# Second-layer modulation as sums on VectorE, and a router that multiplies before the norm, in a two-layer hybrid block with experts

## The chip, the core and the metric

The kernel runs on one core of a Trainium2 chip. The metric is the device time of one execution in microseconds (us); smaller is better. All data are 32-bit floats. The engines that matter here are TensorE (PE; its weight loads are listed as PEld), VectorE (DVE), ScalarE (ACT), GpSimd (POOL) and SyncE (SP), which issues almost all transfers. Each engine works through its own queue in order.

## What is computed

Two layers act on 256 latent tokens and 256 context tokens of width 1024. Cut to what the change touches:

```python
silu_c, silu_cc = silu(c), silu(c_ctx)                     # one vector of 1024 for each stream
m_lat = split(silu_c  @ mod_w[i] + mod_b[i], 6)            # mod_w[i]: 1024 x 6144, 25 MB a layer
m_ctx = split(silu_cc @ mod_w[i] + mod_b[i], 6)
z_lat = modulate(rmsnorm(x, norm1_g[i]), m_lat[0], m_lat[1]) @ w_in[i]
x = x + m_lat[2] * merge(z_lat, att_lat)                   # mixer: pooling, Hyena, attention, w_out
# layer 0: dense SwiGLU on both streams.  layer 1: experts on the latents alone:
u = modulate(rmsnorm(x, norm2_g[1]), m_lat[3], m_lat[4])   # u = x * r * a + b
logits = u @ router_w                                      # 1024 x 8; top 2 of 8 experts for each token
x = x + m_lat[5] * experts(u, logits)
```

The last layer needs the context stream only for its first norm, so of its six modulation vectors only shift and scale of the mixer (column tiles 0 to 3 below) are used for both streams.

## The kernel before

Activations lie transposed: `self.x[j]` holds stream j (0 latents, 1 context) as eight blocks of 128 features by 256 tokens. A product in full precision is made of three products of split operands (`three`, L269): a weight block `raw` (128x1024) is loaded, ACT rounds it to `wh` (L262) and DVE subtracts to get `wl` (L263), and TensorE then runs 24 matmuls of 128x512 for one block (L272 to L274), called a projection here. The ring of `raw` tiles has seven buffers and is shared with the modulation weights (`modw`, same tag); `wh` and `wl` have four buffers each, so weights are prepared up to three projections ahead. PSUM has three tags: `mm` (3 buffers), `aux` (2), `sc` (3).

The modulation weights of a layer are 12 column tiles of 512, each loaded as four chunks (q = 0 to 3) of 128x1024 (two slices of 128 input features, k). In a chunk, four matmuls with the 32 columns of `cvec` as stationary operand (silu of c, silu of c_ctx and zeros) and 256 weight columns moving go to four column groups of the array (`modulation_part`, L353). After the fourth chunk of a tile, `modulation_row` copies the sums to SBUF on ACT (L360), transposes them in two blocks on TensorE (L363), and adds halves and bias on DVE (L367, L369) into `modT`. Ten tiles of layer 0 are done before and inside the first mixer. The last two of layer 0 and all twelve of layer 1 are `self.chunks`: 56 chunks, of which `mod_chunk` takes one after each projection of the dense SwiGLU. There `up` makes gate and up projections for 22 feature blocks, and `down` (called after blocks 8 and 16 and at the end) runs eight output blocks, whose sums DVE adds to both streams (L839).

After the second mixer, `to_experts` (L1363) computes the affine, the norm `r` (`rstd`: Ln, Exp and Square on ACT, three operations on DVE), then eight blocks `xf[k]` = x * r * a + b (DVE L1369; the second step on ACT L1371 for k < 5, on DVE L1373 for the rest), and `logits` multiplies them by the router in four column groups (L915), copies the sums (L917), transposes them (L920) and adds the groups (L923). `route` finds the top two (L935 to L948), `token_major` transposes `xf`, `gather` collects each expert's tokens (L1038), and `experts` streams 336 MB of expert weights through 16 buffers (`mraw`) with the matmuls of L1136, L1147, L1177 and L1185.

The order on each engine is made by a scheduler when the program is built. It follows data dependences and buffer reuse, so the listings of order further down show what it chose.

Of the kernel before, what the change touches and what calls it, by code (L numbers as in the profile page):

```python
# [18 lines left out]
F32 = mybir.dt.float32  # L19
# [3 lines left out]
OP = mybir.AluOpType  # L23
AX = mybir.AxisListType

P = 128
D = 1024
KD = D // P
L = 256
# [5 lines left out]
NE = 8  # L35
EPS = 1e-6
MAGIC = 1.5 * 2.0 ** 23
PAD = 8
# [157 lines left out]
class Trunk:  # L196
# [130 lines left out]
    def conditioning(self):  # L327

        nc = self.nc
        lo = self.par_at["c"][0]  # L330
        both = self.pars[:, lo:lo + 2 * KD]
        sc = self.keep.tile([P, 2 * KD], F32, name="silu_c")
        nc.scalar.activation(sc, both, AF.Exp, scale=-1.0)
        nc.vector.tensor_scalar(sc, sc, 1.0, None, op0=OP.add)
        nc.vector.reciprocal(sc, sc)
        nc.vector.tensor_mul(sc, sc, both)
        self.cvec = self.pre.tile([P, KD, 32], F32, name="cvec")
        nc.gpsimd.memset(self.cvec, 0.0)
        for j in range(2):
            nc.vector.tensor_copy(self.cvec[:, :, j], sc[:, j * KD:(j + 1) * KD])  # L340
# [51 lines left out]
    def mod_chunk(self):  # L392

        if not self.chunks:
            return
        l, ct, q = self.chunks.pop(0)
        if q == 0:
            self.mod_ps = self.sc()
        self.modulation_part(self.mod_ps, q, self.modulation_load(l, ct, q))
        if q == 3:  # L400
            self.modulation_row(l, ct, self.mod_ps, self.aux)

    def mod_chunks_until(self, l, ct):
        while self.chunks and self.chunks[0][:2] < (l, ct):
            self.mod_chunk()
# [499 lines left out]
        down(16, 6, then)  # L905


    def logits(self, xf):

        nc = self.nc  # L910
        ps = self.sc(L)
        rw = self.par("router").rearrange("p (k e) -> p k e", k=KD)
        for k in range(KD):
            g = 32 * (k % 4)
            nc.tensor.matmul(ps[g:g + 32], rw[:, k], xf[k], start=k < 4, stop=k >= 4, tile_position=(0, g))  # L915
        parts = self.tmp("t2", w=L)
        s = nc.scalar.copy(parts, ps)  # L917
        pt = self.sc(L)
        for t in range(2):
            m = nc.tensor.transpose(pt[:, t * P:(t + 1) * P], parts[:, t * P:(t + 1) * P], self.ident)  # L920
        self.routed = m.ins, s.ins
        lg = self.keep.tile([P, 2, NE], F32, name="lg")
        nc.vector.tensor_reduce(lg, pt.rearrange("p (t g e) -> p t e g", t=2, g=4)[:, :, :NE], axis=AX.X, op=OP.add)  # L923
        return lg

    def route(self, lg, between):
# [376 lines left out]
    def run(self, upto=99):  # L1303
        nc, tc = self.nc, self.tc
        with ExitStack() as es:
            self.load(es)
            with ExitStack() as pre:
# [37 lines left out]
                nxt = {}  # L1345
# [15 lines left out]
                xf = []  # L1361

                def to_experts(j):  # L1363
                    a, b = self.affine(1, 2)
                    r = self.norm(0)
                    pairs = [self.block(f"v{k}", T) for k in range(4)]
                    xf.extend(pairs[k // 2][:, k % 2 * L:(k % 2 + 1) * L] for k in range(KD))
                    for k in range(KD):
                        v = nc.vector.tensor_mul(xf[k], self.x[0][:, k], r)  # L1369
                        if k < 5:  # L1370
                            s = nc.scalar.activation(xf[k], xf[k], AF.Identity, bias=b[:, k, 0:1], scale=a[:, k, 0:1])  # L1371
                        else:
                            v = nc.vector.tensor_scalar(xf[k], xf[k], a[:, k, 0:1], b[:, k, 0:1], op0=OP.mult, op1=OP.add)  # L1373
                    nxt["xf"] = v.ins, s.ins
                    nxt["lg"] = self.logits(xf)

                self.merge(0, ym, T, to_dense)
                self.dump("x1", [x[:, k] for x in self.x for k in range(KD)])
# [7 lines left out]
                self.open_blocks(pre, False)  # L1386
                ym = self.mixer(1, self.xm, nxt["mixer"])
                self.merge(1, ym, L, to_experts)
                self.dump("x3", [self.x[0][:, k] for k in range(KD)])
            self.deep.append(es.enter_context(pool("deep1", "left")))  # L1390
# [53 lines left out]
```

## Time and profile before

| what | value |
|---|---|
| median of three runs | 1745.84 us (1744.97 to 1749.46) |
| the profiled execution: its own time | 1746.36 us |
| its span, first to last instruction | 1743.9 us |
| PE busy | 1672.5 us (96%) |
| DVE busy | 608.8 us (35%) |
| ACT busy | 444.2 us (25%) |
| mean DMA rate | 273 GB/s |

The stages, in us from the start of the span: first conditioning and norms to about 60, the first mixer to about 260, w_out and the dense SwiGLU to about 730, the second mixer with its w_out to 879, the router and the gather to 902, the experts to 1738. Busy time is an average over these stages; which wait ends last in each has to be read from that stage. In rows of the timeline, "x8" means that so many instructions in a row were merged into one line, and a matmul of 32-bit floats appears as two instructions (two passes); the start of the next row tells when the engine got on.

### The profile page before, as it was taken

How to read it: one execution, taken by the hardware profiler on the slowest of the kernel's cores; microseconds unless marked ns; L12 is line 12 of the kernel's file. 1: busy time of each engine (PE TensorE's matmuls, PEld its weight loads, DVE VectorE, ACT ScalarE, POOL GpSimd, SP SyncE). 2: the span in 40 equal slices, each digit the busy share in tenths (PEclk: the TensorE clock that was granted, in tenths of full speed). 3: DMA queues.
4: the chain of work that ended last, by engine and by line, in shares of the span. 5: the costliest groups of instructions: out<-in, count | busy, mean ns of one | idle time of the engine just before them, and what ended most of it. 6: DMA issues, size and time to landing. Idle time of an engine off the chain costs nothing. (4 is left out here: it accounts for less than half of the span.)

```text
span 1743.9 us, 27710 instructions
## 1 busy us (share of the span) xinstructions
PE 1672.5 (96%) x11718; PEld 1107.2 (63%) x11718; DVE 608.8 (35%) x1352; ACT 444.2 (25%) x866; POOL 29.4 (2%) x38
## 2 busy tenths in 40 slices
PE   6999999999999999999979999999999999999977
PEld 3777568877777777887755555555555555556533
DVE  5645785533332333768740110221103111031103
ACT  4444464422122122546620100110001000010101
POOL 0021000000000000011000000000000000000000
PEclk8999999999999999999989999999999999999999
DMA  8531262455555554532549999999999999999995
GB/s 302 179 107 58 84 255 73 158 157 169 169 164 165 160 165 132 181 109 85 194 166 387 394 390 423 425 382 422 414 402 426 423 424 408 425 424 425 425 425 239
DMA packets 86314, 475.92 MB, mean 273 GB/s; under 512 B 9708, under 2 KB 13069, under 8 KB 43149
## 3 DMA queue, kind: packets, MB, share of 16 engines
q1 hardware_dynamic: 85580, 473.12, 70.4%
q8 instruction: 121, 1.98, 0.4%
q10 hardware_dynamic: 576, 0.52, 0.1%
q14 instruction: 37, 0.30, 0.1%
HBM read 472.55 MB, written 1.05 MB: 272 GB/s over the span
## 5 line engine op out<-in xcount | busy, mean ns | idle before, releaser
L1136 PE MATMUL mm<-mraw,xg 128*64 128x256 f32 x3584 | 407.8, 381 | 16.4 <-DMA mraw<-in_eg_dram 6.7
L1136 PEld LDWEIGHTS mm<-mraw,xg 128*64 128x64 f32 x3584 | 277.9, 137 | 152.8 <-issue 30.3
L272 PE MATMUL mm<-xh,wh 128*128 128x512 f32 (+1 forms) x656 | 240.8, 368 | 0.8 <-ACT wh L262 0.4
L274 PE MATMUL mm<-xh,wl 128*128 128x512 f32 (+1 forms) x656 | 237.6, 363 | 0.3 <-DVE wl L263 0.3
L273 PE MATMUL mm<-xl,wh 128*128 128x512 f32 (+1 forms) x656 | 237.6, 363 | 0.1
L262 ACT CAST wh<-raw 128x1024 fp32r<-128x1024 f32 (+1 forms) x124 | 128.0, 1034 | 362.6 <-PE mm L273 342.4
L263 DVE TENSOR_TENSOR wl<-raw,wh 128x1024 fp32r<-128x1024 f32 (+1 forms) x124 | 149.9, 1211 | 139.8 <-ACT wh L262 138.1
L1153 DVE TENSOR_TENSOR h<-h,mm 128x256 f32<-128x256 f32 x56 | 23.6, 421 | 408.2 <-ACT h L1152 408.1
L272 PEld LDWEIGHTS mm<-xh,wh 128*128 128x128 f32 x656 | 122.9, 188 | 37.0 <-issue 16.5
L274 PEld LDWEIGHTS mm<-xh,wl 128*128 128x128 f32 x656 | 123.2, 188 | 22.0 <-issue 2.2
L273 PEld LDWEIGHTS mm<-xl,wh 128*128 128x128 f32 x656 | 123.1, 188 | 18.9 <-issue 1.5
L1152 ACT ACTIVATE h<-mm 128x256 f32<-128x256 f32 x56 | 21.5, 383 | 415.7 <-PE mm L1136 415.6
L1185 PE MATMUL sc<-mraw,ht 128*64 128x512 f32 x448 | 109.1, 603 | 3.9 <-PEq L1192 1.9
L1185 PE MATMUL mm<-mraw,ht 128*64 128x512 f32 x448 | 108.8, 603 | 3.4 <-DMA mraw<-in_ed_dram 1.5
L1156 DVE TENSOR_TENSOR hx<-hx,sc 64x256 f32<-64x256 f32 x56 | 23.8, 425 | 232.0 <-ACT hx L1155 231.9
L1155 ACT ACTIVATE hx<-sc 64x256 f32<-64x256 f32 x56 | 21.0, 375 | 259.3 <-PE sc L1147 165.5
L1147 PE MATMUL sc<-mraw,xg 128*32 128x256 f32 x1344 | 76.4, 379 | 0.0
L1185 PEld LDWEIGHTS sc<-mraw,ht 128*64 128x64 f32 x448 | 28.9, 136 | 56.3 <-issue 39.4
L1185 PEld LDWEIGHTS mm<-mraw,ht 128*64 128x64 f32 x448 | 29.1, 136 | 52.1 <-issue 42.3
L1147 PEld LDWEIGHTS sc<-mraw,xg 128*32 128x32 f32 x1344 | 43.4, 110 | 29.5 <-issue 1.2
L839 DVE SCALAR_TENSOR_TENSOR x_latents<-mm,modT,x_latents 128x256 f32<-128x256 f32 x40 | 18.6, 481 | 95.7 <-PE mm L274 95.7
L353 PE MATMUL sc<-modw,cvec 128*32 128x256 f32 x576 | 45.0, 396 | 3.0 <-DMA modw<-in_mod_dram 2.9
(330 smaller groups left out, 2004.2 us busy)
## 6 DMA issues: line engine op xcount, KB each, us to landing
mraw<-in_eg_dram SPq DMA_DIRECT2D x112, 1024.0 KB, 14.4
mraw<-in_eu_dram SPq DMA_DIRECT2D x112, 1024.0 KB, 17.9
mraw<-in_ed_dram SPq DMA_DIRECT2D x112, 1024.0 KB, 11.1
modw<-in_mod_dram SPq DMA_DIRECT2D x96, 512.0 KB, 3.8
raw<-in_win_dram SPq DMA_DIRECT2D x40, 512.0 KB, 4.0
raw<-in_fg_dram SPq DMA_DIRECT2D x22, 512.0 KB, 4.6
raw<-in_fu_dram SPq DMA_DIRECT2D x22, 512.0 KB, 4.5
raw<-in_wout_dram SPq DMA_DIRECT2D x16, 512.0 KB, 4.2
```

Source lines behind the costliest of these rows:

```text
L262: nc.scalar.copy(hi, raw)
L263: nc.vector.tensor_sub(lo, raw, hi.bitcast(F32))
L272: mm(ps, w[0], x[0], start=start, stop=False)
L273: mm(ps, w[0], x[1], start=False, stop=False)
L274: mm(ps, w[1], x[0], start=False, stop=stop)
L353: self.nc.tensor.matmul(ps[g:g + 32, :L], self.cvec[:, 2 * q + k], w[:, k * 512 + n * L:k * 512 + (n + 1) * L], start=q == 0, stop=q == 3, ...
L1136: last = mm(pm[MAIN * j:MAIN * (j + 1), i * L:(i + 1) * L], xg[:, k, :MAIN], r, start=k == 0, stop=k == KD - 1, tile_position=(0, MAIN * j))
L1147: mm(px[q:q + EXTRA], xg[:, k, MAIN:], r, start=k == 0, stop=k == KD - 1, tile_position=(0, q))
L1152: nc.scalar.activation(h, pm[:, :L], AF.Silu)
L1153: nc.vector.tensor_mul(h, h, pm[:, L:])
L1156: nc.vector.tensor_mul(hx[64:], hx[64:], px[64:])
L1185: mm(pds[e % 2][n * MAIN:(n + 1) * MAIN], ht[:, c:c + MAIN], r[:, at + n * 512:at + (n + 1) * 512], start=ft == 0 and k == 0, stop=ft == N ...
```

## The change

Layer 0 keeps its form. For a chunk of layer 1, DVE multiplies each of the two 128x512 slices of the weights by a column of silu(c), one number for each partition, and adds it to a running sum `acc` (128x512): one sum for each stream in the tiles 0 to 3, one sum for the latents alone in the other eight. After a tile's fourth chunk, TensorE sums `acc` over the partitions with four matmuls whose stationary operand is a 128x128 block of `acc` and whose moving operand is one column of ones, and DVE adds the bias. The sums live in the buffers of the pooling mixer (`pz`, `pa`; one buffer each).

The router multiplies u_k = a_k * x_k, before `r` is known; the sums are then multiplied by `r`, and the contribution of the shift b (the same for all tokens) is computed apart and added to the logits. The products `xf` are made as before, for the experts alone.

```diff
@@ mod_chunk @@
         l, ct, q = self.chunks.pop(0)
+        if l == 1:
+            return self.mod_sums(ct, q)
...
+    def mod_sums(self, ct, q):
+        nc = self.nc
+        streams = 2 if ct < 4 else 1
+        if q == 0:
+            wide = [self.temps.tile([P, 2, L + 2 * PAD], F32, name=self.name(n), tag=n, bufs=1) for n in ("pz", "pa")[:streams]]
+            self.sums = [t.rearrange("p s t -> p (s t)")[:, :512] for t in wide]
+        w = self.modulation_load(1, ct, q)
+        for k in range(2):
+            wk = w[:, k * 512:(k + 1) * 512]
+            for j, acc in enumerate(self.sums):
+                c = j * KD + 2 * q + k
+                c = self.silu_c[:, c:c + 1]
+                if q == k == 0:
+                    nc.vector.tensor_scalar(acc, wk, c, None, op0=OP.mult)
+                else:
+                    nc.vector.scalar_tensor_tensor(acc, wk, c, acc, op0=OP.mult, op1=OP.add)
+        if q == 3:
+            ps = self.aux(8)
+            for j, acc in enumerate(self.sums):
+                for b in range(4):
+                    nc.tensor.matmul(ps[:, 4 * j + b:4 * j + b + 1], acc[:, b * P:(b + 1) * P], self.ones[:, 0:1],
+                                     start=True, stop=True)
+            m, mb = self.modT[1][:, 4 * ct:4 * ct + 4], self.par("mod_b1")[:, 4 * ct:4 * ct + 4]
+            for j in range(2):
+                at = 4 * j if streams == 2 else 0
+                nc.vector.tensor_add(m[:, :, j], ps[:, at:at + 4], mb)
@@ logits @@
+    def logit_shift(self, b):
+        nc = self.nc
         rw = self.par("router").rearrange("p (k e) -> p k e", k=KD)
+        n = rw.shape[2]
+        t = self.tmp("t2", w=KD * n)
+        t3 = t.rearrange("p (k e) -> p k e", k=KD)
+        nc.vector.tensor_mul(t3, rw, b[:, :, 0:1].to_broadcast([P, KD, n]))
+        s = self.keep.tile([P, NE], F32, name="shift")
+        nc.vector.tensor_reduce(s, t.rearrange("p (k e) -> p e k", k=KD)[:, :NE], axis=AX.X, op=OP.add)
+        ps = self.aux(NE)
+        nc.tensor.matmul(ps, self.ones, s, start=True, stop=True)
+        self.shift = self.keep.tile([P, NE], F32, name="shift_all")
+        nc.vector.tensor_copy(self.shift, ps)
+
+    def logit_part(self, k, a):
...
+        u = self.tmp("t2", w=L)
+        nc.vector.tensor_scalar(u, self.x[0][:, k], a[:, k, 0:1], None, op0=OP.mult)
+        g = 32 * (k % 4)
+        nc.tensor.matmul(self.lps[g:g + 32], rw[:, k], u, start=k < 4, stop=k >= 4, tile_position=(0, g))
+
+    def logits(self, r):
+        nc = self.nc
         parts = self.tmp("t2", w=L)
-        s = nc.scalar.copy(parts, ps)
+        s = nc.vector.tensor_mul(parts, self.lps, r)
...
         nc.vector.tensor_reduce(lg, pt.rearrange("p (t g e) -> p t e g", t=2, g=4)[:, :, :NE], axis=AX.X, op=OP.add)
+        nc.vector.tensor_add(lg, lg, self.shift.unsqueeze(1).to_broadcast([P, 2, NE]))
@@ to_experts @@
                     a, b = self.affine(1, 2)
+                    self.logit_shift(b)
+                    for k in range(KD):
+                        self.logit_part(k, a)
                     r = self.norm(0)
+                    nxt["lg"] = self.logits(r)
...
-                    nxt["lg"] = self.logits(xf)
```

Three places in the built programs. The first is TensorE's queue in the dense stage, around the end of the third layer-1 tile (column tile 1): the last matmuls of one projection, the two groups of four matmuls with one moving column, and the next projection.

```order
L274 MATMUL mm_3810<-hy_720_3550,wl_3807 128x512
L428 MATMUL aux_3841<-tab_ones,pz_3716 128x1 x4
L428 MATMUL aux_3841<-tab_ones,pa_3717 128x1 x4
L272 MATMUL mm_3860<-q_623_2987,wh_3856 128x512
L273 MATMUL mm_3860<-q_624_2988,wh_3856 128x512
```

Before, four groups like `L353 MATMUL sc<-modw,cvec 32x256 x4` stood in that stretch, one behind each projection, and the two transposes of L363 some matmuls later; now TensorE has nothing of layer 1's modulation until a tile's fourth chunk.

The second place is DVE's queue in the same stretch, a `down` call with two-stream tiles (`mm_...` is the projection whose sums are added to the streams; `pz` and `pa` are the running sums).

```order
L871 SCALAR_TENSOR_TENSOR x_latents<-mm_3810,modT_73,x_latents 128x256
L433 TENSOR_TENSOR modT_74<-aux_3841,pars 128x4 x2
L871 SCALAR_TENSOR_TENSOR x_context<-mm_3810,modT_73,x_context 128x256
L421 TENSOR_SCALAR pz_3885<-modw_3887,silu_c 128x512
L421 TENSOR_SCALAR pa_3886<-modw_3887,silu_c 128x512
L423 SCALAR_TENSOR_TENSOR pz_3885<-modw_3887,silu_c,pz_3885 128x512
L423 SCALAR_TENSOR_TENSOR pa_3886<-modw_3887,silu_c,pa_3886 128x512
L423 SCALAR_TENSOR_TENSOR pz_3885<-modw_3926,silu_c,pz_3885 128x512
L423 SCALAR_TENSOR_TENSOR pa_3886<-modw_3926,silu_c,pa_3886 128x512
L423 SCALAR_TENSOR_TENSOR pz_3885<-modw_3926,silu_c,pz_3885 128x512
L423 SCALAR_TENSOR_TENSOR pa_3886<-modw_3926,silu_c,pa_3886 128x512
L871 SCALAR_TENSOR_TENSOR x_latents<-mm_3860,modT_73,x_latents 128x256
```

In the program before, the same queue holds between two such pairs of adds only the `wl` of a later weight and, once a tile, the three small operations of L367 and L369. Now up to eight operations on running sums stand between two pairs, and each `wl` stands behind some of them.

The third place is DVE's queue in the router, from the last adds to the residual (L871, before L839) to the first step of the top two (L989, before L935).

```order
L962 TENSOR_SCALAR t2_1442_7360<-x_latents_63,affa_1433_7333 128x256
L282 TENSOR_SCALAR rv_1445_7369<-aux_1430_7322 128x256
L962 TENSOR_SCALAR t2_1443_7363<-x_latents_63,affa_1433_7333 128x256
L962 TENSOR_SCALAR t2_1444_7366<-x_latents_63,affa_1433_7333 128x256
L285 SCALAR_TENSOR_TENSOR rz_1447_7371<-rz_1447_7371,rv_1445_7369 128x256
L286 SCALAR_TENSOR_TENSOR ry_1446_7370<-rz_1447_7371,ry_1446_7370 128x256
L970 TENSOR_TENSOR t2_1448_7378<-sc_1436_7344,ry_1446_7370 128x256
L1427 TENSOR_TENSOR v0_1450_7386<-x_latents_63,ry_1446_7370 128x256 x2
L976 TENSOR_REDUCE lg_7383<-sc_1449_7380 128x16
L1427 TENSOR_TENSOR v1_1451_7387<-x_latents_63,ry_1446_7370 128x256
L977 TENSOR_TENSOR lg_7383<-lg_7383,shift_all_7342 128x16
L1427 TENSOR_TENSOR v1_1451_7387<-x_latents_63,ry_1446_7370 128x256
```

Four more products of L1427 (the former L1369) and the three of L1431 (the former L1373) follow, and only then L989. Four products u (L962) stand ahead of the first row shown, behind the last adds. Before, the queue went from the adds straight to L282, then L285, L286, the eight and three operations for `xf`, and only after them L923 and L935.

## Rows read from the trace of the kernel before

**Rows 1.** Busy time by engine (us, instructions), clock and DMA, 378 to 678 us.

```profile
core 0: us, PE busy (x) PEld busy (x) DVE busy (x) ACT busy (x) POOL busy (x), PEclk, DMA share, GB/s
378.00:678.00 300.00, 300.00 (x1538) 217.79 (x1537) 95.47 (x149) 69.79 (x91) 0.00 (x0) 1.00 0.53 162
```

**Rows 2.** The same stretch, instructions of L353 alone.

```profile
378.00:678.00 300.00, 30.67 (x384) 7.55 (x384) 1.00 0.53 162
```

**Rows 3.** Timeline of PE: from one chunk to the next (start, us, instruction).

```profile
403.58 0.64 PE L353 MATMUL sc<-modw,cvec 128*32 128x256 f32 x8
...
404.96 0.39 PE L272 MATMUL mm<-xh,wh 128*128 128x512 f32 x1
...
409.08 0.39 PE L272 MATMUL mm<-xh,wh 128*128 128x512 f32 x1
...
409.86 0.64 PE L353 MATMUL sc<-modw,cvec 128*32 128x256 f32 x8
```

**Rows 4.** Timeline of PE: the two transposes at the end of a tile.

```profile
346.87 0.39 PE L274 MATMUL mm<-xh,wl 128*128 128x512 f32 x1
...
347.10 0.38 PE L363 MATMUL aux<-tab_ident,t 128*128 128x128 f32 x2
...
347.55 0.39 PE L273 MATMUL mm<-xl,wh 128*128 128x512 f32 x1
```

**Rows 5.** Timeline of PE, first stage: four matmuls with one moving column, twice.

```profile
59.97 0.28 PE L273 MATMUL mm<-xl,wh 128*128 128x256 f32 x1
60.29 1.05 PE L475 MATMUL sc<-tab_ones,t 128*128 128x1 f32 x8
61.27 1.12 PE L462 MATMUL sc<-v,q 64*128 64x512 f32 x2
...
64.20 0.95 PE L475 MATMUL sc<-tab_ones,t 128*128 128x1 f32 x8
65.01 0.68 PE L485 MATMUL sc<-k,tab_st 128*128 128x256 f32 x2
```

**Rows 6.** Busy time by engine around them, with the granted clock.

```profile
60.00:66.00 6.00, 5.95 (x36) 4.60 (x35) 2.81 (x11) 1.52 (x4) 0.00 (x0) 1.00 0.53 196
```

**Rows 7.** Groups on DVE by form (busy us, mean ns, idle before).

```profile
L263 DVE TENSOR_TENSOR wl<-raw,wh 128x1024 fp32r<-128x1024 f32 x116 | 142.3, 1229 | 130.9 <-ACT wh L262 129.1
...
L839 DVE SCALAR_TENSOR_TENSOR x_latents<-mm,modT,x_latents 128x256 f32<-128x256 f32 x40 | 18.6, 481 | 95.7 <-PE mm L274 95.7
...
L622 DVE SCALAR_TENSOR_TENSOR e<-e,st 128x512 f32<-128x512 f32 x16 | 11.9, 743 | 0.0
...
L621 DVE TENSOR_SCALAR e<-e,st 128x256 f32<-128x256 f32 x8 | 2.8, 350 | 0.1
```

**Rows 8.** The page's costliest groups: ACT's rounding of weights.

```profile
L262 ACT CAST wh<-raw 128x1024 fp32r<-128x1024 f32 (+1 forms) x124 | 128.0, 1034 | 362.6 <-PE mm L273 342.4
```

**Rows 9.** Timeline of the router, from the last residual to the top two.

```profile
877.98 1.27 DVE L839 SCALAR_TENSOR_TENSOR x_latents<-mm,modT,x_latents 128x256 f32<-128x256 f32 x3 [5.58 <-PE mm L274]
...
881.47 0.42 DVE L282 TENSOR_SCALAR rv<-aux 128x256 f32<-128x256 f32 x1 [2.23 <-ACT ry L281]
...
882.83 0.43 DVE L286 SCALAR_TENSOR_TENSOR ry<-rz,ry 128x256 f32<-128x256 f32 x1
883.29 2.44 DVE L1369 TENSOR_TENSOR v<-x_latents,ry 128x256 f32<-128x256 f32 x7
...
884.40 3.87 PE L915 MATMUL sc<-v,pars 128*32 128x256 f32 x16 [3.47 <-ACT v L1371]
...
888.73 0.55 PE L920 MATMUL sc<-tab_ident,t 128*128 128x128 f32 x2 [0.46 <-ACT t L917]
...
889.32 0.23 DVE L923 TENSOR_REDUCE lg<-sc 128x16 f32<-128x64 f32 x1 [2.17 <-PE sc L920]
889.58 0.17 DVE L935 TENSOR_REDUCE top<-lg 128x2 f32<-128x16 f32 x1
```

**Rows 10.** Timeline of PE: the first two steps of the experts.

```profile
902.21 8.81 PE L1136 MATMUL mm<-mraw,xg 128*64 128x256 f32 x64 [2.00 <-PEq L1192]
...
916.02 7.13 PE L1136 MATMUL mm<-mraw,xg 128*64 128x256 f32 x64 [1.41 <-DVE h L1153]
```

**Rows 11.** Busy time, clock and DMA just ahead of the experts.

```profile
890.00:900.00 10.00, 7.34 (x50) 6.99 (x48) 6.84 (x28) 2.86 (x7) 0.00 (x0) 0.83 0.00 0
```

More of the change, by code (lines that the diff above doesn't have):

```diff
@@ L336, in conditioning @@
         nc.vector.tensor_mul(sc, sc, both)
+        self.silu_c = sc
         self.cvec = self.pre.tile([P, KD, 32], F32, name="cvec")
@@ L905, in dense @@
         down(16, 6, then)
-    def logits(self, xf):
+    def logit_shift(self, b):
         nc = self.nc
-        ps = self.sc(L)
         rw = self.par("router").rearrange("p (k e) -> p k e", k=KD)
-        for k in range(KD):
-            g = 32 * (k % 4)
-            nc.tensor.matmul(ps[g:g + 32], rw[:, k], xf[k], start=k < 4, stop=k >= 4, tile_position=(0, g))
+        n = rw.shape[2]
[10 more added lines that the diff above has]
+        nc = self.nc
+        if k == 0:
+            self.lps = self.sc(L)
+        rw = self.par("router").rearrange("p (k e) -> p k e", k=KD)
+        u = self.tmp("t2", w=L)
[4 more added lines that the diff above has]
+        nc = self.nc
         parts = self.tmp("t2", w=L)
-        s = nc.scalar.copy(parts, ps)
+        s = nc.vector.tensor_mul(parts, self.lps, r)
         pt = self.sc(L)
```

## The prediction

> **What bounds the kernel now.** I read the stage tables first, then the timeline inside the two stages that the change touches, then the groups of DVE. From 378 to 678 us, the stretch of layer 1's modulation, TensorE is busy for all of the 300 us at full clock, while DVE works 95 us and ACT 70 [rows 1]. The list of waits shows none of TensorE there. So this stretch lasts as long as TensorE's queue: what leaves the queue shortens it, what enters lengthens it. That the other engines run ahead is seen on ACT: 342 of its 363 us of idle time before a weight rounding end when TensorE gives a buffer free [rows 8], so weights are ready and wait for room. The router is the opposite, a chain in which one engine waits for the next: DVE for ACT, ACT for DVE, PE for ACT, DVE for PE [rows 9]. No byte is moved from 890 to 900 [rows 11]: the weight buffers of the experts are full and their stage begins when the gather lets it. So microseconds saved in either stage shift the rest as a whole, whatever bounds the experts.
>
> **What leaves TensorE.** 384 instructions of L353 lie in the stretch [rows 2]; a chunk has eight, so these are the 48 chunks of layer 1. From the start of one chunk to the next is 6.28 us, and in between the 24 matmuls keep a cadence of (409.08 - 404.96)/18 = 0.229 us, 5.49 for the projection [rows 3]. A chunk costs 0.79 us; over all such pairs I find 0.76 to 0.78 and use 0.78, hence 37.4 us. The busy time of those rows alone, 30.7 us [rows 2], misses what switching to and from them costs. The two transposes of a tile put 0.68 us between an L274 and the second matmul after it, where 0.46 is usual [rows 4]: 0.22, and 2.7 for twelve tiles. Together 40.1 us go. The copies on ACT go too and give nothing, since nobody waited for ACT.
>
> **What enters TensorE.** Four tiles get eight matmuls with one moving column, eight tiles four: 64, in 16 groups of four. The same form ran before, four matmuls at a time (128x128 of 32-bit floats stationary, a column of ones moving), at full clock [rows 5, 6]. Inside a run of other 32-bit products, four of them held the queue from 64.20 to 65.01, 0.81 us. Behind a stream of short split products, the usual next start would have been 60.09 and the next row started at 61.27: 1.18. So a group costs 0.81 and entering from a stream 0.37 more. Sixteen groups make 13.0, twelve entries 4.4: 17.4 us. Bounds are 13.0 (entries free) and 18.9 (every group at 1.18).
> What the Trainium skill says of it (page "TensorE: Matmul & The Clock Gate", section "Back-to-back issue gap") speaks for less: up to 64 moving columns an isolated matmul takes only an issue floor of some 25 ns. By it the 128 passes would take 3.2 us, and the new time would be some 10 us lower than mine. Its section "LDWEIGHTS" prices the load of 128 columns at about 107 ns whatever the moving side is, and the traced 0.10 us for each of eight passes [rows 5] agrees with that section and not with the floor. The chunks that leave loaded only 32 columns at a time, so this rule speaks against the change.
>
> **What enters DVE.** A chunk of two streams is four operations on 128x512 at 0.743 us, 2.97 us; a chunk of one stream half of that. The nearest row has this form exactly [rows 7]; the first operation of each sum is cheaper and is counted at the same price. DVE is tightest in the first `down` call, all of whose eight chunks have two streams: 1.23 for `wl`, 2 x 0.48 for the streams, 2.97 for the sums, 5.16 us for each projection of 5.5 [rows 3, 7]. It fits by 0.3 us, if nothing else holds the queue. Two new waits do: a tile's first multiplication, or the bias addition ahead of it, waits for the one-column matmuls of the tile before, and behind it stand the next sums, the additions to the streams and `wl`. Walking the printed order with these durations, the worst case is a `wl` finished some 5 us before TensorE needs it, against about 15 us when weights run three projections ahead; and the additions free an `mm` buffer some 3 us before its next use. The cover holds, and I cost this at nothing; without cover a two-stream projection would last as long as DVE's share plus its waits, up to 0.6 us more in each of 16, 10 us. A chunk's buffer is now freed by DVE and not by TensorE; its load stands on SP ahead of the next weight, which is late only if DVE is several projections late.
>
> **The router.** Removed: the products no longer wait for the norm, and no ACT copy stands ahead of the transposes. Added on DVE: eight u at 0.35 us [rows 7], a product with `r`, the addition of the shift. Two u stand ahead of the last adds, where DVE waited 5.6 us anyway. A small copy and four u stand between the adds, which end at 879.25, and L282, where DVE idled 2.23 us [rows 9]: 1.56 us, which fits. But u has two buffers, so each u from the third waits for the product two before it; those stand in TensorE's queue behind sums of squares that ACT must square first. I bound the delay of `r` by 0 and 1.4 us. From `r` (883.26) to the first step of the top two (889.58) it took 6.3 us [rows 9]. Now it takes the product 0.42, transposes and reduction 0.85, and then, since the printed order puts them ahead, the rest of the `xf` work: eleven operations, less the two in the shadow of the transposes, at 0.35 to 0.45, and the addition of the shift, 0.17: 3.3 to 4.2. That is 4.6 to 5.5, so the top two begin between 1.7 us earlier and 0.6 later; I take 0.6 earlier. The gather hangs on the selection as before. The shift's two small operations (under 0.7 us) lie ahead of the last attention output, which w_out uses last, behind seven other blocks; uncovered they would cost 0.7.
> The clock can move it: the first step of the experts took 8.81 us and the next one 7.13, the same 64 instructions [rows 10], with a granted clock of 0.83 around the gather [rows 11], some of it at the lower of the two levels. TensorE now works where it idled and idles where it worked, so such a stretch can fall elsewhere: 1.7 us either way, taken as nothing.
>
> **The sum.** The profiled execution took 1746.36 us, 0.5 above the median. 1746.4 - 40.1 + 17.4 - 0.6 = 1723.1; I predict 1723.5 us, 1.3% less. With its own bounds (40.1 less 13.0 to 18.9; router -1.7 to +0.6; clock 1.7 each way) the likeliest case lies from 1716 to 1727.
>
> **Rivals.**
> - *Cheap one-column matmuls.* If their weight loads hid under the stream's products, as the stream's own loads do, the 13.0 us of the passes could vanish and leave the entries: 1710, or 1716.5 at half of that. Against it speak the traced runs [rows 5], though neither lies in a stream of 512 columns. Chance 0.07. The issue floor of the Trainium skill's page "TensorE: Matmul & The Clock Gate" (section "Back-to-back issue gap") would lead here.
> - *DVE becomes the bound in places.* If it holds weights or `mm` buffers back during the two-stream tiles, 3 to 10 us come back: 1726 to 1734. For it speaks 5.16 of 5.5 us; against it the three projections of lead, and that 32 of the 48 chunks are light. Chance 0.14.
> - *DVE gives it all back.* The same place, at a higher price: DVE decides from (5.5 - 2.19)/4 = 0.83 us for an operation, and all 23 us are lost at 1.45 more for each of 16 projections, 1.19 us for each operation. Traced at 0.743 [rows 7], this needs waits in DVE's queue of another size than I find. Then 1750 or more. Chance 0.03.
> - *It does not do what it says.* The one-column matmuls cost what the chunks did, 0.63 us each (40.1/64), because their switching is dearer in this stream than in the first stage: 1743 to 1748. Twice to three times the traced price. Chance 0.04.
>
> My forecast keeps 0.72. A range that leaves out no more than 2 in 10 reaches from 1715 (half of the first rival) to 1732 (most of the second). A measurement of this kernel can tell about 0.3%, 5 us, from no change: faster than 1740.6 holds for all but the last two rivals and a remainder, 0.92; same 0.05; slower 0.03.
>
> **What would show it.** Right: the stretch that held 48 chunks is 22 to 24 us shorter; TensorE still without waits there; groups of L428 take 0.8 to 1.2 us for four; L423 takes 0.74; DVE's share rises by about 95 us (128 operations); DVE's wait ahead of L282 shrinks and L989 comes about 0.6 us sooner after the last add. Wrong: TensorE waits for `wl` or for an `mm` buffer between the eighth and the 24th chunk; L428 at another price; the experts' first step at another clock.

## The result

The changed kernel takes 1728.78 us (median of four runs, 1725.99 to 1731.52), the kernel before 1747.65 (four runs, 1744.97 to 1749.79): ratio 0.9893, 95% interval 0.9869 to 0.9917, 18.9 us or 1.1% less. The prediction said 1723.5 in a range of 1715 to 1732. In profiled executions the gain is smaller, 1743.9 to 1729.7 us of span; where it came from and went is read by leads: how much sooner an operation of the changed kernel starts than the same one before.

| the same operation in both traces | before | after | lead |
|---|---|---|---|
| first product of squares after the first w_out (L523, now L555) | 293.16 | 292.82 | 0.34 |
| the same at the end of the dense stage | 711.00 | 685.32 | 25.68 |
| first of the last three adds to the residual (L839, now L871) | 877.98 | 857.15 | 20.83 |
| first step of the experts (L1136, now L1190) | 902.21 | 882.04 | 20.17 |
| end of the span | 1743.9 | 1729.7 | 14.2 |

So 25.3 us were won in the dense stage, and 11.5 were lost behind it: 4.8 in the second mixer, 0.7 up to the experts, and 6.0 in the experts, which the change does not touch.

**Dense stage.** Windows of the changed kernel: all engines over the stretch that answers to [rows 1], then TensorE's instructions of L428 alone.

```profile
378.00:655.00 277.00, 277.00 (x1268) 228.26 (x1268) 166.40 (x252) 66.93 (x80) 0.00 (x0) 1.00 0.52 169
```

```profile
378.00:655.00 277.00, 14.94 (x128) 16.14 (x128) 1.00 0.52 169
```

TensorE is still busy throughout, DVE went from a third to 60%. The queue of TensorE where it meets two groups, and further down one (timeline; start, us):

```profile
394.07 0.39 PE L274 MATMUL mm<-xh,wl 128*128 128x512 f32 x1
394.30 0.94 PE L428 MATMUL aux<-tab_ones,pz 128*128 128x1 f32 x8
395.11 1.03 PE L428 MATMUL aux<-tab_ones,pa 128*128 128x1 f32 x8
396.00 0.47 PE L272 MATMUL mm<-xh,wh 128*128 128x512 f32 x1
396.31 0.39 PE L273 MATMUL mm<-xl,wh 128*128 128x512 f32 x1
...
490.07 0.40 PE L274 MATMUL mm<-xh,wl 128*128 128x512 f32 x1
490.31 0.95 PE L428 MATMUL aux<-tab_ones,pz 128*128 128x1 f32 x8
491.12 0.49 PE L272 MATMUL mm<-xh,wh 128*128 128x512 f32 x1
491.44 0.40 PE L273 MATMUL mm<-xl,wh 128*128 128x512 f32 x1
```

The groups start 0.81 apart and hold the queue for 0.81 and 0.89; entering them costs nothing (394.30 is 0.23 after 394.07, the stream's own cadence), leaving them 0.08 (0.31 in place of 0.23). DVE's sums cost what the nearest form cost in [rows 7] (groups: busy us, mean ns, idle before):

```profile
L423 DVE SCALAR_TENSOR_TENSOR pz<-modw,silu_c,pz 128x512 f32<-128x512 f32 x84 | 62.8, 748 | 3.4 <-DMA modw<-in_mod_dram 2.4
L423 DVE SCALAR_TENSOR_TENSOR pa<-modw,silu_c,pa 128x512 f32<-128x512 f32 x28 | 20.9, 745 | 0.0
```

In the waits of 378 to 655 us, DVE's wait for the one-column matmuls is there, and no row has TensorE waiting:

```profile
ACT wh L262 <- PE mm L273: 204.4, 46, 6.3
...
DVE modT L433 <- PE aux L428: 26.5, 12, 4.3
...
DVE pz L421 <- PE aux L428: 3.6, 1, 3.6
```

**Second mixer.** The lead falls from 25.1 to 21.1 us between 817 and 831 us, and nowhere else in this stage by more than 0.6. The granted clock in that window is the lower of the two levels, 1.2 GHz (first row); in a second execution of the same kernel (e3 below, second row) it is the higher one:

```profile
817.40:831.00 13.60, 12.20 (x42) 8.67 (x41) 8.50 (x28) 7.50 (x20) 0.00 (x0) 0.51 0.23 97
```

```profile
817.40:831.00 13.60, 11.27 (x70) 8.56 (x71) 11.02 (x33) 8.47 (x23) 0.00 (x0) 1.00 0.21 87
```

**Router.** Timeline of the changed kernel, for [rows 9]:

```profile
857.15 1.27 DVE L871 SCALAR_TENSOR_TENSOR x_latents<-mm,modT,x_latents 128x256 f32<-128x256 f32 x3 [5.76 <-PE mm L274]
...
861.22 0.61 DVE L962 TENSOR_SCALAR t<-x_latents,affa 128x256 f32<-128x256 f32 x2 [0.83 <-PE sc L964]
...
862.55 0.42 DVE L282 TENSOR_SCALAR rv<-aux 128x256 f32<-128x256 f32 x1
...
862.88 0.82 DVE L962 TENSOR_SCALAR t<-x_latents,affa 128x256 f32<-128x256 f32 x2
...
863.61 0.42 DVE L285 SCALAR_TENSOR_TENSOR rz<-rz,rv 128x256 f32<-128x256 f32 x1
...
864.06 0.43 DVE L286 SCALAR_TENSOR_TENSOR ry<-rz,ry 128x256 f32<-128x256 f32 x1
...
866.07 0.17 DVE L977 TENSOR_TENSOR lg<-lg,shift_all 128x16 f32<-128x16 f32 x1
...
868.92 0.16 DVE L989 TENSOR_REDUCE top<-lg 128x2 f32<-128x16 f32 x1
```

Counted from the first add, the norm starts its last operation at 6.91 us (4.85 before) and the top two begin at 11.77 (11.60 before). The logits are ready at 866.24, and the top two wait 2.7 us behind `xf` on DVE.

**Experts.** From the first step to the end 847.7 us, 841.7 before. The later half is bound by DMA (share 1.01), and there the rate is 419 GB/s, where before it was 425 over the same window (first row: before; second: after):

```profile
1500.00:1690.00 190.00, 176.19 (x1336) 99.32 (x1332) 31.00 (x82) 21.43 (x52) 0.00 (x0) 1.00 1.01 425
1500.00:1690.00 190.00, 170.97 (x1278) 92.11 (x1276) 30.59 (x81) 20.73 (x51) 0.00 (x0) 1.00 1.01 419
```

### The profile page after: what moved, and what is told of

Same layout as the page of the kernel before. It is cut to its first block, busy times and chain, and to the rows that moved or that the text cites. A ratio compares the mean times of both kernels' runs of the same rounds, so it can differ in the third digit from the quotient of the medians.

```text
span 1729.7 us, 27293 instructions
## 1 busy us (share of the span) xinstructions
PE 1657.9 (96%) x11440; PEld 1120.3 (65%) x11440; DVE 692.2 (40%) x1481; ACT 441.1 (26%) x853; POOL 29.1 (2%) x38
## 5 line engine op out<-in xcount | busy, mean ns | idle before, releaser
L1190 PE MATMUL mm<-mraw,xg 128*64 128x256 f32 x3584 | 411.1, 383 | 17.7 <-DMA mraw<-in_eu_dram 7.5
L1190 PEld LDWEIGHTS mm<-mraw,xg 128*64 128x64 f32 x3584 | 276.3, 138 | 159.2 <-issue 31.2
L272 PEld LDWEIGHTS mm<-xh,wh 128*128 128x128 f32 x656 | 123.0, 188 | 24.7 <-issue 2.9
L1210 DVE TENSOR_TENSOR hx<-hx,sc 64x256 f32<-64x256 f32 x56 | 23.8, 424 | 226.4 <-ACT hx L1209 226.3
L1209 ACT ACTIVATE hx<-sc 64x256 f32<-64x256 f32 x56 | 21.1, 376 | 253.7 <-PE sc L1201 166.2
L423 DVE SCALAR_TENSOR_TENSOR pz<-modw,silu_c,pz 128x512 f32<-128x512 f32 x84 | 62.8, 748 | 3.4 <-DMA modw<-in_mod_dram 2.4
L643 PE MATMUL sc<-k,q 64*128 64x512 f32 (+1 forms) x96 | 40.0, 580 | 2.0 <-DVE k L632 1.6
```

Of the source, the lines that this page charges most:

```text
L272: mm(ps, w[0], x[0], start=start, stop=False)
L423: nc.vector.scalar_tensor_tensor(acc, wk, c, acc, op0=OP.mult, op1=OP.add)
L643: nc.tensor.matmul(s[m], q[h][r, qs], k[h][r, k0:k0 + nk], start=True, stop=True)
L1190: last = mm(pm[MAIN * j:MAIN * (j + 1), i * L:(i + 1) * L], xg[:, k, :MAIN], r, start=k == 0, stop=k == KD - 1, tile_position=(0, MAIN * j))
L1210: nc.vector.tensor_mul(hx[64:], hx[64:], px[64:])
```

## The experiments

Theory: the sums are worth what the dense stage shows, the router next to nothing, and the 6 us in the experts come from something that the change moved without meaning to. Rival: they are chance, like the clock in the second mixer, or the router's own.

Measured (medians in us, 4 to 6 runs each and 12 of e9; ratio to the kernel before in the same group of runs; the three stretches from one profiled execution each: the dense stage between the first two operations of the table above, the router from the first add to the experts' first step, the experts from there to the end):

| kernel | median | ratio, 95% interval | dense | router | experts | GB/s, 1500 to 1690 |
|---|---|---|---|---|---|---|
| before | 1746.3 to 1748.7 (four groups of runs) | 1 | 417.8 | 24.2 | 841.7 | 425 |
| after | 1728.8 | 0.9893 [0.9869, 0.9917] | 392.5 | 24.9 | 847.7 | 419 |
| e1 | 1720.0 | 0.9844 [0.9831, 0.9858] | 392.2 | 24.1 | 840.0 | 425 |
| e2 | 1755.2 | 1.0050 [1.0035, 1.0065] | 417.7 | 24.5 | 846.3 | 419 |
| e3 | 1727.3 | 0.9893 [0.9878, 0.9908] | 392.5 | 25.5 | 846.1 | 419 |
| e4 | 1725.9 | 0.9883 [0.9869, 0.9898] | 392.2 | 23.8 | 845.1 | 419 |
| e5 | 1727.5 | 0.9886 [0.9867, 0.9905] | 392.5 | 25.4 | 844.7 | 419 |
| e6 | 1724.7 | 0.9871 [0.9852, 0.9890] | 392.3 | 23.9 | 843.8 | 420 |
| e7 | 1720.5 | 0.9840 [0.9824, 0.9857] | 390.7 | 24.7 | 839.0 | 425 |
| e8 | 1719.0 | 0.9834 [0.9818, 0.9850] | 392.2 | 25.5 | 839.4 | 425 |
| e9 | 1748.1 | 1.0009 [0.9995, 1.0023] | 412.9 | 25.6 | 845.8 | 419 |
| e10 | 1735.8 | 0.9938 [0.9920, 0.9956] | 402.8 | 25.4 | 845.8 | 419 |
| e11 | 1717.4 | 0.9835 [0.9815, 0.9854] | 390.7 | 24.2 | 840.1 | 425 |
| e12 | 1721.5 | 0.9850 [0.9831, 0.9868] | 390.7 | 23.7 | 842.1 | 425 |

**e1, the sums alone.** The new functions of the router and their calls go, the old ones come back:

```diff
-                    self.logit_shift(b)
-                    for k in range(KD):
-                        self.logit_part(k, a)
                     r = self.norm(0)
-                    nxt["lg"] = self.logits(r)
...
+                    nxt["lg"] = self.logits(xf)
```

> The sums on VectorE alone, the router as in the kernel before. Theory A (the sum of the prediction, with its dense-stage terms as the changed kernel's trace has them): nearly all of the gain is in the dense stage, so the span from the first dense block to the end of the dense stage is 25 us shorter than before (25.3 measured with both parts), and the time is 19 to 25 us under the kernel before, equal to the changed kernel within 2 us. Rival B: the router is worth more than it looks, and the sums alone give under 15 us. On the clock: if the 13.65 us of half granted clock that the changed kernel shows in the second mixer (817.5 to 831.1 us) come with the earlier start of that mixer, they stand here at the same operations; if they are a chance of the one profiled execution, they are absent or elsewhere, and the second mixer then keeps the full lead of 25 us.

1719.97 us, 27.5 under the kernel before: a little more than theory A gave, and 7 to 9 us under the changed kernel, which neither theory had. The half clock stands in the second mixer here too (816.0 to 826.2 us), so it needs no new router; e3 has the same kernel as "after" and lacks it. Experts: 840.0 us.

**e2, the router alone.** The other half of the diff, on the kernel before.

> The router that multiplies before the norm alone, modulation on TensorE as before. The prediction gave this part -0.6 us (bounds -1.7 to +0.6), and the changed kernel's trace showed the top-two 0.17 us later after the first add of the last residual than before. Theory A: within 1.5 us of the kernel before (ratio 0.999 to 1.001). Rival B: the eight scalings on VectorE stand ahead of the norm's last two operations and cost more than the sums by the reciprocal save, time 2 us or more above the kernel before.

7.8 us above the kernel before: rival B by the time, but not by its place. The norm is late as B said (its last operation at 6.91 us after the first add), yet the top two begin at 11.78, as in the changed kernel. What is long is the experts' stage, 846.3 us, with this window:

```profile
1500.00:1690.00 190.00, 175.44 (x1366) 98.50 (x1360) 30.30 (x80) 20.71 (x50) 0.00 (x0) 1.00 1.01 419
```

The two parts multiply to 0.9844 x 1.005 = 0.9893, the ratio of the whole.

**e3, the changed kernel again,** without an edit.

> The changed kernel once more, on the chip of the other runs of this group. Theory A: ratio to the kernel before 0.987 to 0.992 as first timed, and equal to the product of the two parts apart within 0.1%. In its trace: the dense stage 25 us shorter again; the half clock in the second mixer and the experts' stage (847.7 us in the first profile, 841.7 before) differ from the first profile by some us if they vary by execution, and repeat within 1 us if they belong to the kernel.

The same ratio to four digits. The second mixer has no half clock this time, the experts take 846.1 us: the first varies by execution, the second belongs to the kernel.

**e4, the router's weights scaled in place of the residual.**

```diff
-        u = self.tmp("t2", w=L)
-        nc.vector.tensor_scalar(u, self.x[0][:, k], a[:, k, 0:1], None, op0=OP.mult)
+        if k == 0:
+            nc.vector.tensor_mul(rw, rw, a[:, :, 0:1].to_broadcast([P, KD, rw.shape[2]]))
...
-        nc.tensor.matmul(self.lps[g:g + 32], rw[:, k], u, start=k < 4, stop=k >= 4, tile_position=(0, g))
+        nc.tensor.matmul(self.lps[g:g + 32], rw[:, k], self.x[0][:, k], start=k < 4, stop=k >= 4, tile_position=(0, g))
```

> The changed kernel with the router's weights (128 x 8 x 32) scaled by the modulation once, ahead of time, in place of the eight scalings of the residual (8 x 0.35 us on VectorE, and TensorE's waits for them). The norm's operation at L285 waited for these scalings from 862.04 to 863.61 us. Theory A: the norm ends 1.3 to 1.6 us sooner after the first add, the whole router with it, and the time is 1 to 2 us under the changed kernel. Rival B: the top-two stands behind the scaled tokens on VectorE, which has the same work left, so that under 0.5 us is gained.

The first add stands at 853.87; in this timeline the norm's last operation starts 5.38 us later (6.91 with the scalings), the top two 10.23 (11.77):

```profile
859.25 0.42 DVE L286 SCALAR_TENSOR_TENSOR ry<-rz,ry 128x256 f32<-128x256 f32 x1
...
864.10 0.16 DVE L989 TENSOR_REDUCE top<-lg 128x2 f32<-128x16 f32 x1
```

1.5 us sooner, as theory A says; the medians (1727.31 and 1725.88) differ by as much, with intervals that overlap. So the scalings explain 1.5 us, and not the 7.8 that e2 lost.

**e5 and e6, the addresses.** What else came with the router are two tiles of eight numbers, `shift` and `shift_all`, in the pool that lives to the end. They take 64 bytes of each partition, and in the built program 13 of the 16 buffers of the experts' weights move with them, from byte 15104 (a multiple of 256; the others follow at steps of 8192) to 15168. These two kernels are e1 with a dead tile of 16 or 32 numbers:

```diff
         self.modT = [self.keep.tile([P, 48, 2], F32, name=f"modT{l}") for l in range(2)]
+        nc.gpsimd.memset(self.keep.tile([P, 16], F32, name="pad"), 0.0)
```

> The sums alone (e1) with one dead tile of 64 bytes a partition in the pool that holds what lives through the kernel. The new router's two shift tiles add just these 64 bytes, and with them 13 of the 16 buffers of the experts' weights begin 64 bytes later in each partition (byte 15168 in place of 15104: 64 over a multiple of 256 in place of a multiple). Theory A: the addresses cost the 6 us that every kernel with the new router shows after the first expert step (845.2 to 847.7 us there, 840.1 and 841.7 without), at 419 GB/s in place of 425 in the full slices; so this kernel is 5 to 6 us above e1, at 1725 to 1726 us, with 419 GB/s. Rival B: the loss comes with the router's work or its time, and the dead tile changes nothing: 1720 us, 425 GB/s.

> As e5 with a dead tile of 128 bytes: the 13 buffers begin at a multiple of 128 that is none of 256. Theory A with a step of 128 bytes: the rate is 425 GB/s again and the time that of e1, 1720 us. Theory A with a step of 256 bytes or more: as e5, 1725 us and about 419 GB/s. Rival B (addresses don't matter): 1720 us for e5 and e6 alike.

Windows of e1, e5 and e6, in this order:

```profile
1500.00:1690.00 190.00, 172.60 (x1252) 95.80 (x1250) 31.02 (x82) 21.07 (x52) 0.00 (x0) 1.00 1.01 425
```

```profile
1500.00:1690.00 190.00, 170.51 (x1248) 92.19 (x1236) 30.30 (x80) 20.68 (x50) 0.00 (x0) 1.00 1.01 419
```

```profile
1500.00:1690.00 190.00, 169.99 (x1230) 92.51 (x1224) 30.30 (x80) 20.68 (x50) 0.00 (x0) 1.00 1.01 420
```

A tile that nobody reads costs 7.5 us with 64 bytes and 4.7 with 128 (medians against e1's, which ran in another group; the experts' stage is 4.7 and 3.8 us longer). The interval of e6 overlaps that of e1; against e8 below, an aligned kernel of their own group of runs, the two stand 8.5 and 5.7 us higher, and there no intervals overlap. The share of the DMA engines is 1.01 in all three: they are as busy and move less. Rival B falls. The dead tile moves all that lies above it, the experts' activations too; that it is the transfers into the buffers that suffer is read from this rate, as no run moved the buffers alone. A step of 128 bytes would not do either: 128 over a multiple of 256 is slow too.

**e7, the changed kernel with its old addresses.** The two tiles move to a pool that is given back before the experts:

```diff
-        s = self.keep.tile([P, NE], F32, name="shift")
+        s = self.pre.tile([P, NE], F32, name="shift")
...
-        self.shift = self.keep.tile([P, NE], F32, name="shift_all")
+        self.shift = self.pre.tile([P, NE], F32, name="shift_all")
```

> The changed kernel, with its two shift tiles in the pool that is given back ahead of the experts, so that the 16 weight buffers stand where they stood before the change; the operations are the same. Theory A: the stretch from the first expert step to the end is 840 to 842 us in place of 846.1 and 847.7, and the time 5 to 6 us under the changed kernel, 1721 to 1723 us. Rival B: the router itself costs the 7 us, and the time stays at 1727 us.

```profile
1500.00:1690.00 190.00, 173.13 (x1312) 96.35 (x1306) 30.27 (x80) 20.67 (x50) 0.00 (x0) 1.00 1.01 425
```

1720.51 us, 0.9840 [0.9824, 0.9857], and 425 GB/s with the same instructions as the changed kernel. The experts take 839.0 us. This settles the cause from the other side: put the buffers back and the loss is gone. Not all of the time that e7 gains is the experts': its dense stage is 1.8 us shorter than that of the changed kernel, for another reason (last section).

**e8, the other three buffers.** In every kernel so far they begin 224 bytes over a multiple of 256.

```diff
+                nc.gpsimd.memset(es.enter_context(pool("top", "right")).tile([P, 120], F32, name="pad"), 0.0)
                 self.deep = [es.enter_context(pool("deep0", "right"))]
```

> The sums alone (e1), with 480 bytes left free at the top of the partition, so that the other three weight buffers, which begin 96 bytes over a multiple of 128 in every kernel so far, begin at a multiple of 512 too. Theory A: if an unaligned start costs each transfer alike, these three of 16 cost 3/13 of what e5 costs, 1.2 to 1.4 us, and the time is 1718.5 us with 426 to 427 GB/s. Rival B: the start of these three doesn't matter, 1720 us and 425 GB/s.

425 GB/s as in e1, the experts 0.6 us shorter, the median 1 us lower, intervals that overlap: what was expected is too small to be told from nothing here. Left open.

**e9, the one-column groups twice.**

```diff
-            for j, acc in enumerate(self.sums):
+            for j, acc in [*enumerate(self.sums)] * 2:
                 for b in range(4):
```

> The changed kernel with every group of one-column matmuls issued twice into the same sums (128 in place of 64; the output is the same). The prediction put a group of four at 0.81 us and an entry into the stream at 0.37; its rival put a group at 0.06 to 0.2 us. The changed kernel's trace shows groups of four 0.81 apart and entries of about 0.2. Theory A: 16 more groups of 0.81 us lengthen the stretch from the first dense block to the end of the dense stage by 13 us, and the time to 1740 to 1741 us. Rival B (cheap one-column matmuls): 1 to 3 us more, 1729 to 1731 us.

20.8 us above e3 by the medians: more than theory A. The timeline around a tile with two streams, and a window behind it:

```profile
391.68 0.39 PE L274 MATMUL mm<-xh,wl 128*128 128x512 f32 x1
391.91 0.95 PE L428 MATMUL aux<-tab_ones,pz 128*128 128x1 f32 x8
392.72 1.03 PE L428 MATMUL aux<-tab_ones,pa 128*128 128x1 f32 x8
393.61 1.03 PE L428 MATMUL aux<-tab_ones,pz 128*128 128x1 f32 x8
394.50 1.03 PE L428 MATMUL aux<-tab_ones,pa 128*128 128x1 f32 x8
395.40 0.47 PE L272 MATMUL mm<-xh,wh 128*128 128x512 f32 x1
...
396.39 0.63 PE L272 MATMUL mm<-xh,wh 128*128 128x512 f32 x1
396.81 0.63 PE L273 MATMUL mm<-xl,wh 128*128 128x512 f32 x1
```

```profile
396.00:399.40 3.40, 3.40 (x10) 2.68 (x9) 3.40 (x6) 0.00 (x0) 0.00 (x0) 0.51 0.26 57
```

A group in the stream takes 0.81 to 0.90 us. Behind four in a row the granted clock falls to 1.2 GHz for 3.4 us, where the products come 0.43 us apart in place of 0.23; this happens behind each of the four two-stream tiles and nowhere else in the dense stage. In 3.4 us at half clock stand eight products, which else take 1.8, so 1.6 are lost: 6.4 in all, which leaves 20.4 - 6.4 = 14.0 of the dense stage's growth for 16 groups, 0.88 each. Cheap one-column matmuls (rival B) are out.

**e10, VectorE's sums twice.** Behind each sum but a tile's first stands a second operation of the same form that adds nothing.

```diff
                     nc.vector.scalar_tensor_tensor(acc, wk, c, acc, op0=OP.mult, op1=OP.add)
+                    nc.vector.scalar_tensor_tensor(acc, wk, 0.0, acc, op0=OP.mult, op1=OP.add)
```

> The changed kernel with a second operation of the same kind behind each of the 112 sums of VectorE that adds the weight times zero (112 x 0.75 us = 84 us more of VectorE's time; the output is the same). Theory A: the sums cost nothing because VectorE has room; in the part with two sums per chunk (349 to 468 us) the doubled work comes to about 122 of 119 us, just past that room, in the rest it stays under it: the dense stage is 0 to 8 us longer, the time 1727 to 1736 us. Rival B: the sums already delay the weights' low halves, and doubling them costs a large part of the 84 us, 30 us or more: 1757 us and above.

8.5 us above e3 for 77 us of more work (the added operations took 0.68 to 0.69 us): the time is just inside theory A's range, but the dense stage grew by 10.3 us, past its 8. Windows (the first is the part with two streams) and waits of 378 to 660 us:

```profile
378.00:470.00 92.00, 87.74 (x384) 69.84 (x383) 74.18 (x121) 17.89 (x21) 0.00 (x0) 0.96 0.39 124
470.00:660.00 190.00, 189.21 (x859) 155.67 (x858) 152.10 (x227) 47.33 (x57) 0.00 (x0) 1.00 0.59 187
```

```profile
ACT wh L262 <- DMA raw<-in_fd_dram: 26.3, 5, 6.9
...
PEld mm L274 <- DVE wl L263: 5.3, 6, 1.2
```

With DVE at 81% of the first window TensorE is idle for 4.3 us of it; at 80% of the second for 0.8. The rest of the 10.3 us by which the dense stage grew holds two pieces of 3.4 us at half clock, some 3.2 us lost; 2.0 us stay unexplained. ACT now waits for weights that come late, since the chunks' buffers are freed late, as the prediction described: in SP's own list of waits over this stretch, its issues of weight loads (L259) wait 112.2 us for the sums of DVE; in the changed kernel it was 86.3 (378 to 655 us). So there was room for the single sums, and less than twice as much in the two-stream part.

**e11, both repairs** (e4 and e7 together).

> The sums, and the router of e4 (weights scaled once, ahead of time) with the shift tiles placed as in e7, so that the weight buffers stand where they stood. Expected from the parts: e7 measured 1720.5 us, and e4's norm came 1.53 us sooner after the first add of the last residual (5.38 in place of 6.91 us): 1719 us. If the addresses are not the cause of what the new router lost, it stays at e4's 1726 us.

1717.44 us, ratio 0.9835 [0.9815, 0.9854]: below both kernels, 10 to 11 us below the changed one (e3 and the first timing). Against e1, e7 and e8 the intervals overlap.

**e12, the top two ahead of half of `xf`.** On top of e11; the routing's tiles move to the pool that lives to the end, and 192 dead bytes bring the 13 buffers to multiples of 512:

```diff
+                    tokens(range(4))
+                    self.route(nxt["lg"], lambda part: tokens(range(4, KD)))
...
-            self.route(nxt["lg"], rest)
+            rest(0)
```

> As e11, and the top-two on VectorE ahead of the last four tokens' blocks, with the tiles of the routing in the pool that lives through the kernel, and 192 dead bytes there so that the 13 buffers begin at multiples of 512 bytes. The top-two starts right after its sums, 1.5 to 2 us sooner after the first add than in e4 (10.23 us), the gather 0.5 to 1.5 us sooner than there (14.95). Theory A on addresses: 425 GB/s in the full slices, as at multiples of 256, and 1717 to 1718.5 us. Rival: multiples of 512 are better than of 256 (13 buffers of 16), over 427 GB/s and under 1715 us.

The steps came as expected (top two 7.81 us after the first add, gather 13.55), the time did not: 1721.45, 4 us above e11. One difference is seen in its window of the gather:

```profile
863.00:883.00 20.00, 17.29 (x76) 13.70 (x77) 12.18 (x48) 6.18 (x12) 0.00 (x0) 0.50 0.66 263
```

The granted clock is at its lower level from 862.5 to 882.9 us, through the whole gather and the first steps of the experts; in e11 it is 0.68 over 859 to 880. Only 0.6 us of 2.4 reach the experts' first step, and their stage is 2.1 us longer. The first stage also held 6.8 us more of half clock in this execution than in e11, and the second mixer 3.4 more. All five runs of e12 have a mean clock of 0.984 to 0.986, those of e11 0.986 to 0.988; whether the order makes the clock fall was not separated from chance. Multiples of 512 give 425 GB/s, like multiples of 256.

## Why the prediction was right, and what it missed

The time lies in its range, 5.3 us above its value. It also lies 1.8 us above the likeliest case (1716 to 1727) and among the times of the rival in which DVE becomes the bound in places (1726 to 1734), but that rival is not what happened: no wait of TensorE for DVE shows in the stretch. That the range holds is in part luck, since its biggest miss, 5.9 us in the experts, stood in no term and in no rival. Against the sum, 1723.1, the errors are -2.6 us in the dense stage, +0.8 in the router, +5.9 in the experts and +1.3 in the start, as the kernel before has a median of 1747.65 over four runs where the sum set out from 1746.4: 5.4 of 5.7.

- **What leaves and enters TensorE** (40.1 and 17.4): right in its mechanism, the entry mis-sized. The prediction sized it at 0.37 us from a place of the first stage; in the stream of 512 columns it is 0.08. The group of four, 0.81, held (0.81 to 0.90 here and in e9). By the timeline, two groups hold TensorE for 396.31 - 394.07 - 2 x 0.23 = 1.78 us and one for 0.91, entry and exit included; over the twelve tiles of this trace that is 14.4 us, against 17.4. With the measured 25.3 of the whole stage, 39.7 left, against 40.1. The terms should have come to -25.3 and came to -22.7. The 0.10 us for each pass also agrees with the section "LDWEIGHTS" of the Trainium skill's page "TensorE: Matmul & The Clock Gate", and not with that page's issue floor.
- **DVE costs nothing:** right, at 0.745 to 0.748 us each; the new waits of DVE for the one-column matmuls are there (26.5 us), and no row of the waits from 378 to 655 us has TensorE in it. e10 shows how near the end of the room was.
- **The router** (-0.6): +0.17, inside its bounds, though two parts of it were not. The delay of `r`, bounded by 0 and 1.4 us, was 2.06, from the u that wait for TensorE to free their two buffers; from its end (864.49) to the top two it took 4.43 us, just under the 4.6 to 5.5. e4, which has no u, takes 1.5 of the delay away.
- **The step that failed** in the working, though the range held, is "So microseconds saved in either stage shift the rest as a whole, whatever bounds the experts." That took it that the experts' stage is the same behind the change. It was not: two tiles moved the weight buffers, and the rate fell from 425 to 419 GB/s (e2, e5, e7). The stage's mean over the kernels with the 13 buffers at multiples of 256 is 840.1 us (before, e1, e7, e8, e11; e12 with its low clock left out) and over those 64 bytes above 845.9 (after, e2, e3, e4, e5, e9, e10): a term of +5.9 us that the sum did not have.
- **The clock** (1.7 either way): in this pair of profiled executions it was 4 us, in the second mixer; the experts' first step took 8.78 us after 8.81. Ten of the fourteen traces hold a piece of half clock in the second mixer, and it is absent from the one the prediction read, from e3, e8 and e10; since it comes and goes in one kernel, these 4 us can't be put down to the change.

Of the signs it named, the stretch came out 25.3 us shorter (22 to 24 said) and DVE's busy time 83.4 us longer (608.8 to 692.2; about 95 said), and the top two came 0.17 us later after the last add, not 0.6 sooner. None of those for a wrong forecast showed.

The terms as measured, -25.3 + 0.2 + 5.9 = -19.2 us, stand beside the 18.9 of the medians.

On the addresses, the Trainium skill's page "DMA: Bandwidth & Descriptors", section "How a descriptor splits into AXI transactions", says that a transaction (one of the pieces into which a transfer's descriptor is split) must start at a multiple of 256 bytes; a descriptor that starts elsewhere begins with one from the boundary below, and the bytes ahead of its start are fetched unused and still cost time. It speaks of fetching, whereas here it is the destinations that moved. The step of 256 agrees with e1, e5, e6 and e12. The sizes don't: worked out from that section's beats of 32 bytes, an estimate for 8192 bytes is 2 beats more on 256 for a start 64 over and 4 for 128 over, 0.8 and 1.6%, and measured are 1.4% (419) and 1.2% (420).

## What to carry to other kernels

Before a tile is added to a pool that lies under large transfer buffers, see where those buffers begin afterwards, and keep them at multiples of 256 bytes; a stage that no line of the change touches can lose 6 us by it. To move reductions from TensorE to an idle VectorE pays where TensorE's queue is the stage, but the last sum over partitions keeps its price: some 0.9 us here for 512 columns, as four 32-bit matmuls with one moving column. Time the parts of a change apart: one of these two was a loss, hidden behind the other's gain.

## What was not expected of the hardware

- The start of a buffer in the partition changes the rate of the weight stream: 425 GB/s at multiples of 256 bytes, 419 at 64 above, 420 at 128 above, with the DMA share at 1.01 in each.
- In e9, sixteen matmuls with one moving column in a row (3.5 us) were followed by 3.4 us at half clock in a stream that did not wait, four times in four; the eight in a row of the changed kernel never were. In e10 two such pieces stand where TensorE waited for DVE soon after a tile's groups.
- The place of half-clock pieces varies between executions of one kernel, in the first stage, the second mixer and the gather, and goes with most of the spread of some 5 us: runs of the kernel before with a mean clock of 0.992 took 1743.7 to 1745.0 us, those with 0.987 1747.4 to 1751.3.
- In e7, e11 and e12 the dense stage takes 390.7 us, in the seven others with the single sums 392.2 to 392.5, and the difference grows evenly along the stage. What the three share is that, in the built programs, the split weights (`wh`, `wl`) stand 64 bytes further from the normed activations than in the seven. Other ways to tell this apart were not tried; it stays open.
